# Seven-product FFN tiles: high and low token parts in one matmul, weight totals prepared in DRAM or added by DMA, and a written order

## The chip, the cores and the metric

The kernel runs on one core of a Trainium2 chip. Its time is device microseconds for one launch; three runs gave 2419.32, 2420.54 and 2422.15 us (median 2420.54). The engines are PE (TensorE, matmul; PEld is its weight load), DVE (VectorE), ACT (ScalarE), POOL (GpSimd) and SP (SyncE, which here only issues DMAs). POOL and ACT issue DMAs too; in this kernel the DMAs that add to what stands at their destination are all POOL's.

## The reference

Two layers of an encoder on 512 tokens of width 1024. Each layer has a half-step FFN, a mixer, and another half-step FFN; the change is in the FFNs.

```python
def swiglu(h, w_gate, w_up, w_down):
    return (jax.nn.silu(h @ w_gate) * (h @ w_up)) @ w_down
...
h = rms_norm(x, norm_g[l, 0])
x = x + 0.5 * swiglu(h, ffn_w_gate[l, 0], ffn_w_up[l, 0], ffn_w_down[l, 0])
```

The mixer projects the normalized tokens, runs three kinds of attention beside each other (2-D neighbourhood, differential, windowed with shared keys), gates and merges their outputs, and adds the result to x. The FFN's inner width is 2816, that is 22 tiles of 128 columns.

## The kernel before, in words

**Split numbers.** Everything that TensorE multiplies is split into a high part (rounded to fp32r on ACT) and a low part (the rest, a subtraction on DVE). A product is three matmuls per block of 128 inputs: high weights with high tokens, high weights with low tokens, low weights with high tokens. `parted` (L91) splits a 128x1024 weight tile: one ACT copy (L95) and one DVE subtraction (L96). `weights` (L80) loads a tile and does the same (L86 to L88). Both draw the parts from rings of four buffers (`whi`, `wlo`), and the loaded tile from a ring of three (`raw`).

**The four FFNs.** For each of the 22 tiles `ffn` (L275) computes gate and up. The first two tiles of an FFN (the first four in the first FFN) are plain: 24 matmuls of 512 columns each for gate and for up (`product`, L105), and `gated` (L360) makes silu(gate) times up. During them `Sides` (L368) prepares sums and differences of token blocks. All later tiles, 18 in the first FFN and 20 in each of the other three, go through `seven` (L418).

**A seven-product tile.** Gate and up of one tile are one product of a 2x2 block matrix of weights with a 2x2 block matrix of tokens, and it is done in seven block products instead of eight (Strassen's scheme in Winograd's form). Each block product multiplies 512 inputs with 256 token columns: `block_product` (L456) issues eight matmuls with the high weights (L460, L461) and four with the low ones (L463), all 256 columns wide. The weights of the seven products are: two halves of the raw tile (`wa`), two halves of gate plus up (`w31`, from `wsum`), one quarter of up (`w22`, from `a22`), and two halves of a further total (`w24`). `wsum` is made by two DMAs (`added`, L408): SP loads gate's columns, POOL's DMA adds the up tile (L415). `w24`'s input is made on DVE by two additions of 128x512 into the raw tile (L446, L447), and then parted. The partial sums are gathered from PSUM by ACT copies (L474, L483, L485) and DVE additions (L487, L490, L491); then come the gate's scaling (L494), Silu on ACT (L495), the product (L496) and the split of the result (`keep`, L119 and L121).

**What sets the order.** Within the limits of data and buffers, a planner places each engine's instructions by estimated costs; `tc.issue_after` adds single order constraints. Each engine then works through its list in that order.

**After the tiles** come eight tiles of the down projection (L336 to L348: 66 matmuls of 512 columns each); in the last FFN `finish` (L599) takes their place. The mixer (L666) calls `weights` some 70 times per layer, and POOL in it builds bias tiles (L876, L926) and issues small DMAs, among them the swapped queries `qks` (L700, L701), which the score matmuls read.

## Time and profile before

| what | value |
|---|---|
| three runs | 2419.32, 2420.54, 2422.15 us |
| profiled execution: first to last instruction (its own time; the profile gives no other) | 2419.2 us |
| seven-product tiles of the four FFNs | 54.7 to 238.2, 888.9 to 1090.5, 1233.7 to 1435.3, 2085.9 to 2287.5 us |
| mixers, roughly | 360 to 830 and 1555 to 2030 us |
| busy: PE, DVE, ACT, POOL | 99%, 68%, 52%, 11% |
| granted TensorE clock, mean | 0.998 |
| HBM read, written | 302.69 MB, 12.62 MB |

A row of the timeline has the start in us, the duration in us (a count after it if several are merged), the engine, the line, the operation, what is written and read, and in brackets the idle time before it and what ended that. Matmul records overlap: a matmul's duration runs from its start to the modelled end of its results, and the next one starts well before that. What a matmul costs in a stream is the distance from its start to the next start. The same holds, less strongly, for DVE and ACT. For a DMA the profile gives the time from its issue to its landing.

### The profile page before, as it was taken

To read this page: it belongs to the slowest core of one execution; us is meant where nothing else is said; L and a number is where in the kernel's file an instruction comes from. 1 tells how busy PE (TensorE), PEld (TensorE's weight loads), DVE (VectorE), ACT (ScalarE), POOL (GpSimd) and SP (SyncE) were. 2 spreads that over 40 slices of the span, in tenths; PEclk is the share of its full clock that TensorE was granted. 3 is DMA by queue.
4 is the path that set the end of the run, shared out by engine and by line. 5 is a ranking of instruction groups with operands and counts; after the bars stand their busy time and mean duration, and the time that the engine had idled before them with its cause. 6 is when DMAs were issued, how large, how long until landed. Compare 5 with 4: busy or idle time off the path is not lost.

```text
span 2419.2 us, 37505 instructions
## 1 busy us (share of the span) xinstructions
PE 2404.9 (99%) x14418; PEld 2138.0 (88%) x14418; DVE 1652.9 (68%) x2767; ACT 1254.9 (52%) x2277; POOL 270.2 (11%) x404
## 2 busy tenths in 40 slices
PE   9999999999999999999999999999999999999998
PEld 7999888888888889998899998888888888999987
DVE  7888445766666678884398873467666666888832
ACT  6555225756567445552255552367566674555532
POOL 3100003311000010000010000133110000100000
PEclk9999999999999999999999999999999999999999
DMA  6675444432332457664367754443322324577632
GB/s 198 174 186 162 128 135 124 115 98 80 94 88 80 131 160 183 185 157 143 119 179 183 183 151 131 127 129 104 101 83 87 95 94 131 168 181 182 175 114 70
DMA packets 113298, 327.19 MB, mean 135 GB/s; under 512 B 13464, under 2 KB 18888, under 8 KB 113120
## 3 DMA queue, kind: packets, MB, share of 16 engines
q1 hardware_dynamic: 88896, 247.04, 33.1%
q0 software_dynamic: 23072, 75.90, 14.4%
q8 instruction: 114, 1.87, 0.3%
q10 hardware_dynamic: 1152, 1.86, 0.2%
q14 instruction: 64, 0.52, 0.1%
HBM read 302.69 MB, written 12.62 MB: 130 GB/s over the span
## 4 chain that ended last, share of the span: by engine, by line
PE 98%; ACT 1%; DVE 0%; issue 0%; DMA 0%; SPq 0%; POOLq 0%; POOL 0%; DVEq 0%; ACTq 0%
PE mm L112 9%; PE mm L110 9%; PE mm L109 9%; PE mm L344 5%; PE mm L345 5%; PE mm L347 5%; PE pr L463 5%; PE pr L460 5%; PE mm L460 5%; PE mm L461 5%; PE mm L463 5%; PE pr L461 5%; PE av L847 2%; PE mm L1065 2%; PE mm L1061 2%; PE mm L1060 2%
## 5 line engine op out<-in xcount | busy, mean ns | idle before, releaser
L87 ACT CAST whi<-raw 128x1024 fp32r<-128x1024 f32 (+1 forms) x258 | 265.7, 1031 | 420.9 <-PE mm L345 184.8
L88 DVE TENSOR_TENSOR wlo<-raw,whi 128x1024 fp32r<-128x1024 f32 (+1 forms) x258 | 309.5, 1201 | 229.1 <-ACT whi L87 121.5
L109 PE MATMUL mm<-h,whi 128*128 128x512 f32 x800 | 318.5, 398 | 0.0
L110 PE MATMUL mm<-l,whi 128*128 128x512 f32 x800 | 313.9, 392 | 0.0
L96 DVE TENSOR_TENSOR wlo<-raw,whi 128x1024 fp32r<-128x1024 f32 x156 | 191.1, 1225 | 83.1 <-ACT whi L95 82.9
L345 PE MATMUL mm<-g,whi 128*128 128x512 f32 x528 | 205.4, 389 | 0.0
L344 PE MATMUL mm<-g,whi 128*128 128x512 f32 x528 | 205.4, 389 | 0.0
L112 PE MATMUL mm<-h,wlo 128*128 128x512 f32 x800 | 197.7, 389 | 0.0
L112 PEld LDWEIGHTS mm<-h,wlo 128*128 128x128 f32 x800 | 150.2, 188 | 31.3
L110 PEld LDWEIGHTS mm<-l,whi 128*128 128x128 f32 x800 | 150.5, 188 | 29.1 <-DVE l L141 0.5
L109 PEld LDWEIGHTS mm<-h,whi 128*128 128x128 f32 x800 | 150.4, 188 | 29.0 <-ACT h L139 0.6
L95 ACT CAST whi<-raw 128x1024 fp32r<-128x1024 f32 x156 | 163.9, 1050 | 10.1 <-DMA raw<-in_w_gu 8.0
L460 PE MATMUL pr<-side,whi 128*128 128x256 f32 x624 | 156.5, 283 | 0.0
L461 PE MATMUL pr<-side,whi 128*128 128x256 f32 x624 | 156.5, 283 | 0.0
L461 PE MATMUL mm<-l,whi 128*128 128x256 f32 x624 | 156.5, 283 | 0.0
L460 PE MATMUL mm<-h,whi 128*128 128x256 f32 x624 | 156.4, 283 | 0.0
L415 POOL DMA_DIRECT2D wsum<-in_w_gu x78 | 68.0, 872 | 686.9 <-DVE g L121 255.7
L347 PE MATMUL mm<-g,wlo 128*128 128x512 f32 x528 | 131.4, 389 | 0.0
L474 ACT COPY gu<-mm 128x256 f32<-128x256 f32 x78 | 29.0, 372 | 195.3 <-PE mm L463 195.2
L806 ACT ACTIVATE lg<-lg,negm 128x256 f32<-128x256 f32 (+1 forms) x192 | 114.2, 595 | 26.7 <-DVE negm L803 25.5
L461 PEld LDWEIGHTS mm<-l,whi 128*128 128x128 f32 x624 | 119.8, 192 | 0.2
L460 PEld LDWEIGHTS mm<-h,whi 128*128 128x128 f32 x624 | 119.8, 192 | 0.2
(306 smaller groups left out, 6130.1 us busy)
## 6 DMA issues: line engine op xcount, KB each, us to landing
raw<-in_w_gu SPq DMA_DIRECT2D x94, 512.0 KB, 3.7
wsum<-in_w_gu SPq DMA_DIRECT2D x78, 512.0 KB, 4.1
wsum<-in_w_gu POOLq DMA_DIRECT2D x78, 512.0 KB, 6.6
raw<-in_w_down SPq DMA_DIRECT2D x48, 512.0 KB, 3.6
raw<-in_w_gate SPq DMA_DIRECT2D x48, 512.0 KB, 3.6
raw<-in_w_qk SPq DMA_DIRECT2D x44, 512.0 KB, 3.6
a<-in_w_gu SPq DMA_DIRECT2D x78, 256.0 KB, 4.8
raw<-in_w_branch SPq DMA_DIRECT2D x24, 512.0 KB, 3.5
```

The lines of the kernel that those rows point to most:

```text
L87: nc.scalar.copy(hi[:, w], raw[:, w])
L88: lower[:] = [nc.vector.tensor_tensor(out=lo[:, w], in0=raw[:, w], in1=f(hi[:, w]), op=ALU.subtract).ins]
L96: nc.vector.tensor_tensor(out=lo, in0=src, in1=f(hi), op=ALU.subtract)
L109: nc.tensor.matmul(ps, wh, xhi[k], start=k == 0, stop=False)
L110: nc.tensor.matmul(ps, wh, xlo[k], start=False, stop=False)
L112: nc.tensor.matmul(ps, wl, xhi[k], start=False, stop=k == n - 1)
L344: nc.tensor.matmul(ps, w[k][0], ghi[c + k], start=c + k == 0, stop=False)
L345: nc.tensor.matmul(ps, w[k][0], glo[c + k], start=False, stop=False)
L347: nc.tensor.matmul(ps, w[k][1], ghi[c + k], start=False, stop=c + k == MF - 1)
L460: nc.tensor.matmul(ps, wh[k], bh, start=start and k == 0, stop=False, skip_group_check=True)
L461: nc.tensor.matmul(ps, wh[k], bl, start=False, stop=False, skip_group_check=True)
L463: nc.tensor.matmul(ps, wl[k], bh, start=False, stop=stop and k == 3, skip_group_check=True)
```

## The change

**Joined matmuls.** The high and low parts of the tokens now stand beside each other in one tile ([128, 2, 512], and likewise for the sums and differences). In a "wide" block product one matmul of 2 x 256 columns takes the place of the two with the high weights: the high part's results go to the first half of a PSUM bank, the low part's to the second, and the halves are added later by ACT copies and 256-column DVE additions. The low weights still take 256 columns. Six of the seven products are wide in three FFNs (all but product 1), and products 3, 4 and 5 in the first FFN. A wide product has 8 matmuls instead of 12.

**Weight totals.** For the last three FFNs gate plus up is made ahead, in DRAM, during the mixers (`prepare`): SP copies gate's tile DRAM to DRAM, POOL's DMA adds up's. These steps are handed out by `weights` calls inside the mixer: 40 tiles in the first mixer, 20 in the second. In the tile itself SP loads the finished total. The two additions for `w24` are now two POOL DMAs, SBUF to SBUF, the second on the result of the first; on DVE they remain in the first FFN and in the first tile of each FFN.

**Written order.** Inside `tile` all engines, and the issue of DMAs, follow the order of the program text (`in_order`). Product 4 of a tile, and all that follows from it up to the split of the result (`tail`), is issued inside the next tile, between its products; after the last tile it is issued in the first down tile (or in `finish`). The order of products is 1, 5, 4 of the tile before, 6, 2, 3, 7. The loads of a tile are issued two tiles ahead (one for `a22`). The small tables of the first FFN come inside that order as well.

```diff
+WIDE, WIDE_FIRST = frozenset((2, 3, 4, 5, 6, 7)), frozenset((3, 4, 5))
...
+    owed[0] += owed[1]
+    while ahead and owed[0] >= 1:
+        owed[0] -= 1
+        with tc.issue_after(loaded[0]):
+            if next(ahead[0], ahead) is ahead:
+                ahead.pop(0)
...
-        hi = xpool.tile([P, S], F32R, tag=f"h{k}", name=f"h{k}")
+        both = self.both[k] = xpool.tile([P, 2, S], F32R, tag=f"h{k}", name=f"h{k}")
+        hi, lo = both[:, 0], both[:, 1]
...
+                if m == plain:
+                    tiles = Seven(l, i, h, fp, sides, ghi, glo)
+                    with tc.issue_after(h.marks[1]):
+                        with tc.issue_after(loads[1]):
+                            tiles.fetch(m, sums)
+                        tiles.wa[m] = parted(tiles.raw[m])
+                        tiles.fetch_a22(m)
+                        tiles.fetch(m + 1)
+                        with tc.issue_after(sides[3].mark), tc.issue_after(h.spread):
+                            tiles.w31[m] = parted(sums)
                 with tc.issue_after(h.marks[1]):
-                    held, gated_last = seven(l, i, m, h, fp, sides, ghi, glo, loads[1], sums if m == plain else None, held)
+                    tiles.tile(m)
...
+                if m == 0 and c == 8:
+                    tiles.flush()
...
+        self.t = [two[:, :, :H], two[:, :, H:], both]
+        self.b11, self.b21, self.b22 = h.both[e][:, :, :H], h.both[o][:, :, :H], h.both[o][:, :, H:]
+        self.t4, self.b12 = t4, h.both[e][:, :, H:]
...
+        if (l, i) in prepared:
+            loaded[:] = [nc.sync.dma_start(t, prepared[l, i][m]).ins]
+            return t.rearrange("p n c -> p (n c)")
...
+def prepare(l, i):
+    prepared[l, i] = {}
+    waiting = []
+    def accumulate():
+        t, src = waiting.pop(0)
+        nc.gpsimd.dma_start(t.rearrange("p n c -> p (n c)"), src, accum_op=ALU.add, max_dma_last_dim=4096)
+    for m in range(2, MF):
+        gu = a["w_gu"][l, i, m]
+        t = prepared[l, i][m] = dram.tile([P, 2, S], F32, tag=f"d_s{l}{i}_{m}", name="d_s")
+        nc.sync.dma_start(t, gu.rearrange("n p c -> p n c")[:, :, 0:S])
+        waiting.append((t, gu[1]))
+        if len(waiting) > 2:
+            accumulate()
+        yield
+    while waiting:
+        accumulate()
+        yield
+class Seven:
...
+    @contextmanager
+    def in_order(self):
+        traced = nc.cur_bb.bb.instructions
+        last = traced[-1]
+        yield
+        start = next(k for k in reversed(range(len(traced))) if traced[k] is last) + 1
+        for ins in traced[start:]:
+            if ins.engine in self.behind:
+                why = mybir.DependencyInfo(mybir.DependencyClass.NoSync, mybir.DependencyReason.DATA)
+                tc.add_manual_dep(ins, self.behind[ins.engine].name, why, reason="in_order")
+            self.behind[ins.engine] = ins
+    def fetch(self, m, sums=None):
+        if m >= MF:
+            return
+        (l, i), fp = self.at, self.fp
+        self.sums[m] = sums or added(l, i, m, fp)
+        self.raw[m] = wpool.tile([P, 1024], F32, tag="raw", name="raw", bufs=3)
+        nc.sync.dma_start(self.raw[m], a["w_gu"][l, i, m, 0])
+    def fetch_a22(self, m):
+        if m < MF:
+            self.a22[m] = work.tile([P, S], F32, tag="x", name="a22", bufs=2)
+            nc.sync.dma_start(self.a22[m], a["w_gu"][self.at + (m, 1)][:, S:])
+    def others(self, m, engine):
+        s2, s4 = self.raw[m][:, :S], self.raw[m][:, S:]
+        for out, more in ((s2, self.sums[m][:, S:]), (s4, s2)):
+            if engine is nc.gpsimd:
+                engine.dma_start(out, more, accum_op=ALU.add)
+            else:
+                engine.tensor_tensor(out=out, in0=more, in1=out, op=ALU.add)
+    def product(self, n, bank, w, b, start=False, stop=False):
+        (wh, wl), ps = w, bank[:, 0]
+        for k, bk in enumerate(b):
+            go = start and k == 0
+            if n in self.wide:
+                nc.tensor.matmul(bank, wh[k], bk, start=go, stop=False, skip_group_check=True)
+            else:
+                nc.tensor.matmul(ps, wh[k], bk[:, 0], start=go, stop=False, skip_group_check=True)
+                nc.tensor.matmul(ps, wh[k], bk[:, 1], start=False, stop=False, skip_group_check=True)
+        for k, bk in enumerate(b):
+            nc.tensor.matmul(ps, wl[k], bk[:, 0], start=False, stop=stop and k == 3, skip_group_check=True)
...
+    def tile(self, m):
+        h, fp, sides, last = self.h, self.fp, self.sides, m == MF - 1
+        first = not sides[0].t[3:]
+        tail = iter(self.tail)
+        def rest():
+            for emit in tail:
+                emit()
+                return
...
+        g = quarters(fp)
+        q = [g[:, n] for n in range(5)]
+        one = mm_tile().rearrange("p (a c) -> p a c", a=2)
+        two = psum.tile([P, 2, H], F32, tag="s", name="pr", bufs=2)
+        three = psum.tile([P, 2, H], F32, tag="t", name="pv", bufs=2)
+        wa, w31 = self.wa.pop(m), self.w31.pop(m)
+        w24 = room()
+        with self.in_order():
+            self.fetch(m + 2)
+            self.fetch_a22(m + 1)
+            self.product(1, one, blocks(wa), [s.b11 for s in sides], start=True)
+            rest()
+            if not last:
+                self.wa[m + 1] = room()
+                parted(self.raw[m + 1], self.wa[m + 1])
+                if self.ready:
+                    self.others(m + 1, nc.gpsimd)
+            if first:
+                self.others(m, nc.vector)
+            parted(self.raw.pop(m), w24)
+            rest()
+            u1 = self.halves(1)
+            nc.scalar.copy(g[:, 0:u1], one[:, 0:u1])
+            self.product(5, two, blocks(w31, S), side(1), start=True)
+            rest()
+            if u1 == 2:
+                add(q[0], q[0], q[1])
+            v = self.halves(5)
+            nc.scalar.copy(q[4], two[:, v - 1])
+            if v == 2:
+                add(q[4], two[:, 0], q[4])
+            rest()
+            w22 = [fp.tile([P, S], F32R, tag=t, name=t) for t in ("w22h", "w22l")]
+            a22 = self.a22.pop(m)
+            nc.scalar.copy(w22[0], a22)
+            nc.vector.tensor_tensor(out=w22[1], in0=a22, in1=f(w22[0]), op=ALU.subtract)
+            self.product(6, one, blocks(w24), side(2))
+            u2 = self.halves(1, 6)
+            nc.scalar.copy(g[:, 1 : 1 + u2], one[:, 0:u2])
+            if u2 == 2:
+                add(q[1], q[1], q[2])
+            rest()
+            if first:
+                for s in sides:
+                    s.last()
+            if not last and not self.ready:
+                self.others(m + 1, nc.vector)
+            self.product(2, three, blocks(wa, S), [s.b21 for s in sides], start=True, stop=True)
+            for n in range(self.halves(2)):
+                add(q[0], three[:, n], q[0])
+            if not last:
+                self.w31[m + 1] = room()
+                parted(self.sums.pop(m + 1), self.w31[m + 1])
+            self.product(3, two, blocks(w24, S), [s.b22 for s in sides], stop=True)
+            for n in range(self.halves(3, 5)):
+                add(q[1], two[:, n], q[1])
+            gn = g[:, 0:2].rearrange("p a c -> p (a c)")
+            un = g[:, 3:5].rearrange("p a c -> p (a c)")
+            nc.vector.tensor_tensor(out=gn, in0=gn, in1=h.rb, op=ALU.mult)
+            self.product(7, one, blocks(w31), side(3))
+        u3 = self.halves(1, 6, 7)
+        hi = fp.tile([P, S], F32R, tag="g", name="g", bufs=GBUFS)
+        lo = fp.tile([P, S], F32R, tag="g", name="g", bufs=GBUFS)
+        self.out[0].append(hi)
+        self.out[1].append(lo)
+        def sum22():
+            nc.scalar.copy(g[:, 2 : 2 + u3], one[:, 0:u3])
+            for n in range(u3):
+                add(q[4], q[4], q[2 + n])
+        def gate():
+            nc.scalar.activation(gn, gn, AF.Silu)
+        def fourth():
+            self.product(4, one, blocks(w22), side(4), stop=True)
+        def up():
+            n = self.halves(1, 4, 6, 7)
+            nc.scalar.copy(q[3], one[:, n - 1])
+            if n == 2:
+                add(q[3], one[:, 0], q[3])
+            nc.vector.scalar_tensor_tensor(out=un, in0=un, scalar=-1.0, in1=gn, op0=ALU.mult, op1=ALU.mult)
+        def kept():
+            nc.scalar.copy(hi, un)
+            nc.vector.tensor_tensor(out=lo, in0=un, in1=f(hi), op=ALU.subtract)
+        self.tail = sum22, gate, fourth, up, kept
...
+    ahead[:] = [prepare(*at) for at in ([(0, 1), (1, 0)] if l == 0 else [(1, 1)])]
+    owed[:] = 0.0, 24 * len(ahead) / 72
```

145 lines of the change are left out of this document (49 added, 96 removed).

## The prediction

> **What bounds the kernel now.** I first read the busy shares, the chain of waits, and the table by stretches (us, then busy time and instructions of PE, weight load, DVE, ACT and POOL, granted clock, DMA share, GB/s):
>
> ```profile
> span 2419.2 us, 37505 instructions
> PE 2404.9 (99%) x14418; PEld 2138.0 (88%) x14418; DVE 1652.9 (68%) x2767; ACT 1254.9 (52%) x2277; POOL 270.2 (11%) x404
> PE 98%; ACT 1%; DVE 0%; issue 0%; DMA 0%; SPq 0%; POOLq 0%; POOL 0%; DVEq 0%; ACTq 0%
> ...
> 54.70:238.20 183.50, 182.98 (x1515) 181.78 (x1515) 160.22 (x234) 103.78 (x170) 17.08 (x22) 1.00 0.65 169
> 360.00:830.00 470.00, 469.08 (x2427) 395.29 (x2426) 313.23 (x662) 287.93 (x601) 68.61 (x103) 1.00 0.34 99
> 888.90:1090.50 201.60, 201.60 (x1681) 201.56 (x1680) 175.97 (x243) 112.90 (x184) 16.80 (x20) 1.00 0.67 173
> ```
>
> PE is the bound: almost never idle in the tiles (third and first stretch: 20 tiles of 10.08 us, 18 of 10.19), at full clock. But DVE there is busy 176 of 201.6 us, 87%. So PE time that is taken away counts only until DVE, or something DVE waits for, is the next limit.
>
> A busy PE doesn't yet tell what a matmul costs, since the records overlap. Starts do. PE's timeline, the same product in two successive tiles, and then four 512-column matmuls of the down projection:
>
> ```profile
> 1420.91 0.28 PE L460 MATMUL pv<-h,w22h 128*128 128x256 f32 x1
> 1421.03 0.28 PE L461 MATMUL pv<-l,w22h 128*128 128x256 f32 x1
> ...
> 1430.99 0.28 PE L460 MATMUL pv<-h,w22h 128*128 128x256 f32 x1
> ...
> 1437.84 0.39 PE L345 MATMUL mm<-g,whi 128*128 128x512 f32 x1
> 1438.06 0.39 PE L344 MATMUL mm<-g,whi 128*128 128x512 f32 x1
> 1438.29 0.39 PE L345 MATMUL mm<-g,whi 128*128 128x512 f32 x1
> 1438.52 0.39 PE L344 MATMUL mm<-g,whi 128*128 128x512 f32 x1
> ```
>
> A tile takes 1430.99 - 1420.91 = 10.08 us for 84 matmuls: 0.120 us per 256 columns. At 512 columns it is (1438.52 - 1437.84)/3 = 0.2267 us. The durations in the rows (0.28 and 0.39) would make joining worth 0.17 us a pair; the starts say 2 x 0.120 - 0.2267 = 0.0133 us. The large-looking saving is thirteen times too large.
>
> **The matmuls.** A wide product drops 4 matmuls. Three FFNs: 20 tiles x 6 x 4 x 3 = 1440; the first: 18 x 3 x 4 = 216. Together 1656 x 0.0133 = **22.0 us** less PE time; a tile falls to 9.76 us (a wide product 1.39, product 1 still 1.44), in the first FFN to 9.92. Were joining worth 0.17 us, it would be 280 us; I take the starts, since they add up to the tile's time.
>
> In the Trainium skill, "TensorE: Matmul & The Clock Gate", section "Back-to-back issue gap", a matmul in a stream costs its columns at 2.4 GHz plus 2.5 ns. By that a dropped matmul returns 2.5 ns (an estimate from that page), 1656 of them 4 us, and everything below would turn the change into a loss. This trace differs: 120 ns is 13.3 above 256 columns at that clock, and 227 is 13.3 above 512; the measurement decides.
>
> **DVE and ACT in a tile.** Here too starts count; one tile of DVE, then ACT:
>
> ```profile
> 1393.97 0.42 DVE L487 TENSOR_TENSOR gu<-mm,gu 128x256 f32<-128x256 f32 x1
> 1394.30 1.21 DVE L96 TENSOR_TENSOR wlo<-wsum,whi 128x1024 fp32r<-128x1024 f32 x1
> 1395.44 0.68 DVE L490 TENSOR_TENSOR gu<-pr,gu 128x512 f32<-128x512 f32 x1
> ...
> 1397.24 0.68 DVE L494 TENSOR_TENSOR gu<-gu,rb 128x512 f32<-128x512 f32 x1
> 1397.84 0.68 DVE L447 TENSOR_TENSOR raw<-raw 128x512 f32<-128x512 f32 x1
> ...
> 1391.14 1.05 ACT L95 CAST whi<-raw 128x1024 fp32r<-128x1024 f32 x1
> 1392.09 0.62 ACT L436 CAST w22h<-a 128x512 fp32r<-128x512 f32 x1
> 1392.61 0.37 ACT L485 COPY pv<-pr 128x256 f32<-128x256 f32 x1
> 1392.91 1.04 ACT L95 CAST whi<-wsum 128x1024 fp32r<-128x1024 f32 x1
> ```
>
> DVE needs 1.14 us per 1024 columns, 0.60 per 512, 0.33 per 256; ACT 0.95, 0.52, 0.30. DVE before: three of 1024, eight of 512, one of 256 = 8.55 of 10.08 us. After, in a tile with six wide products: three of 1024, four of 512, nine of 256 (one each for products 1 with 6, 5 and 4, two each for 2, 3 and 7) = 3.42 + 2.40 + 2.97 = 8.79 of 9.76 us. In the first FFN, with L446 and L447 kept and six small additions, 9.0 of 9.92. ACT: 2.85 + 5 x 0.52 + 3 x 0.30 = 6.35. So DVE stays under PE, by a margin reduced from 1.5 to 1.0 us. These additions cost nothing while that cover lasts.
>
> **The two DMA additions.** The input of product 6 (`w24`) now comes from two chained POOL DMAs of 256 KB. Setting the start of a tile to 0, products end at 1.44 (1), 2.83 (5), 4.22 (4 of the tile before), 5.6 (6), 7.0, 8.4, 9.76. On ACT stand first the copy of the last tile's bank (0.2 to 0.7 us), then the rounding of the next tile's raw weights to about 1.8; DVE's subtraction of 1.2 us reads them until 3.0. Only then may the first addition overwrite them. Product 6 of the next tile starts at 9.76 + 4.22 = 13.98; before it ACT must round `w24` (1.05), do the Silu that is queued behind (0.52) and copy product 1 out of product 6's own bank (0.37). So the second addition must land by about 12.0: 9.0 us for two, **4.5 us each**. No such DMA is in the trace. The nearest (KB, median us to landing):
>
> ```profile
> wsum<-in_w_gu POOLq DMA_DIRECT2D x78, 512.0 KB, 6.6
> qks<-qk POOLq DMA_DIRECT2D x72, 128.0 KB, 2.3
> lg<-d_x POOLq DMA_DIRECT2D x16, 256.0 KB, 3.0
> ```
>
> Bounds: 2.3 (half the size, no adding) to 6.6 (twice the size, adding). Plain transfers rise 0.7 from 128 to 256 KB, so plain 512 KB would be 4.4; adding costs 2.2 more there, half of that here: 3.0 + 1.1 = 4.1 us. That is 0.4 us inside the deadline, so it hides; for single late pairs I put 1.2 us in all. At 2.3 us nothing is lost either. With the cover gone, product 6 waits, and behind it all of PE; each us by which one addition exceeds 4.5 us lengthens a tile by about 1 us (both are late, but half is regained, since the next tile's additions start from its raw weights and not from `w24`). At 6.6 that is 60 x 2.1 = 126 us.
>
> **Entry of each FFN.** In its first joined tile product 4 of a tile before is missing, so product 6 is due at 2.83 us, and its input is made on DVE, after the rounding of the next tile's weights. How it looks there now (tile start, then DVE and ACT):
>
> ```profile
> 888.94 0.28 PE L460 MATMUL mm<-h,whi 128*128 128x256 f32 x1
> ...
> 888.37 0.68 DVE L365 TENSOR_TENSOR gu<-pg,gu 128x512 f32<-128x512 f32 x1
> 889.57 0.68 DVE L365 TENSOR_TENSOR gu<-mm,gu 128x512 f32<-128x512 f32 x1
> 891.37 0.68 DVE L121 TENSOR_TENSOR g<-gu,g 128x512 fp32r<-128x512 f32 x1
> 893.51 1.23 DVE L96 TENSOR_TENSOR wlo<-raw,whi 128x1024 fp32r<-128x1024 f32 x1
> ...
> 889.08 0.62 ACT L119 CAST g<-gu 128x512 fp32r<-128x512 f32 x1 [1.11 <-DVE gu L365]
> ```
>
> Now DVE's low part of `w24` ends 5.8 us into the tile, and only the sixth product needs it. After: the next tile's `whi` buffer is the fourth back, that of the last plain product, free at 0.2 us. ACT rounds to 1.25, DVE subtracts to 2.4, adds twice to 3.6, ACT rounds `w24` to 4.7: product 6 waits 2.0 us beyond 2.83, and about 0.3 for the low part. DVE also still owes up to three 512-column steps of the last plain tile (the L365 and L121 rows above), at worst 1.2 us on this path: 2.3 to 3.5. I take 2.6 us x 4 entries = **10.4 us**. PE never regains this. No gain is possible here, since PE loses nothing at this place today; zero is the bound below.
>
> **The preparation in the mixers.** 60 SP copies and 60 POOL additions of 512 KB. A row for all queues' traffic and the price of POOL's part:
>
> ```profile
> q1 hardware_dynamic: 88896, 247.04, 33.1%
> q0 software_dynamic: 23072, 75.90, 14.4%
> ...
> L415 POOL DMA_DIRECT2D wsum<-in_w_gu x78 | 68.0, 872 | 686.9 <-DVE g L121 255.7
> ```
>
> Plain MB cost 0.331 x 2419/247 = 3.24 us of the DMA engines, POOL's 4.6: 4.1 us for one total. 40 totals in the first mixer are 164 of 470 us, and its DMA share goes from 0.34 to about 0.69, no more than the 0.67 at which the tiles above lose nothing. POOL gets 40 x 0.87 = 35 us more beside 69 busy. A weight load behind a copy lands some 2 us later, and is issued a product ahead (24 x 0.227 = 5.4 us); bias builds and swapped queries stand behind additions on POOL's queue. If that cover failed in a third of the cases at 1 us, 20 us; I take 2 us. In the tiles, traffic falls (the total comes in one load instead of two).
>
> **Small tables.** In the first FFN two matmuls now stand in PE's written order and wait for an ACT copy: 1 us, from 0 to 3. Product 4 after the last tile is issued a third into the first down tile (24 x 0.227 = 5.4 us of matmuls before and behind it), longer than its chain: nothing. SP's loads run two tiles ahead: nothing.
>
> **Sum.** 2419.2 - 22.0 + 10.4 + 1.2 + 2 + 1 = 2411.8 us profiled. The runs' median lies 1.3 us above that span, so 2413 us.
>
> **Rivals.**
> - *Nothing lost at the entries*: the planner clears DVE early. For it: DVE has 1.5 us a tile to spare. Against: the written order itself. 2413 - 10 = 2403.
> - *The DMA additions come late*; the slower case. Place: ACT's rounding of `w24`, hence product 6, in 60 tiles. It decides from 4.6 us per addition (60 x 0.12 us eats the 7.4 us gained); at 4.9 us, 60 x 0.4 = 24, less the 1.2 already counted: 2436. For it: 0.4 us is a thin margin, and the loads share the DMA engines. Against: interpolation from three sizes.
> - *The mixers suffer*: 10 us more than I took, 2423.
> - *Joining doesn't do what it says*: moving columns from two separate stretches cost more than the contiguous 512 in the rows, so that a pair takes 0.24 again: 2435. The trace has no such operand in a stream. By the rule of the Trainium skill above it would be 2431; its chance is within this one's.
>
> **How the numbers follow.** Forecast 0.45 (its own range 2406 to 2422), entries free 0.15, late additions 0.2, mixers 0.13, joining worth nothing 0.07. Fewer than 2 in 10 lie outside 2400 (all but the entry cost hidden better than I think) and 2438 (additions at 4.9 us). A measurement tells 0.2% (4.8 us) from no change: faster is below 2415.7, slower above 2425.4. Faster: 0.32 of the forecast's 0.45, and the free entries, 0.47. Slower: 0.16 of the late additions, 0.04 of the mixers, 0.05 of the joining: 0.25. The rest, 0.28, is no change.
>
> **What would show it.** Joined matmuls start 0.227 us apart and a tile lasts 9.76 us: the matmul term holds. PE waits at product 6 for ACT's `w24` only in the first tile of an FFN, 2 to 3.5 us: the entry term. The additions land in about 4.1 us; a PE wait at product 6 in every tile and landings above 4.5 us would be the slower rival. Mixers longer than before with PE waiting for `qks` or raw weights would be the third. I am wrong altogether if DVE, at 90% in a tile, falls behind by itself, shown by PE waiting for DVE where no DMA is late.

## The result, and the profile after

The changed kernel takes **2436.86 us** (median of 4 runs, 2434.38 to 2449.10), the kernel before 2419.93 in the runs beside it: a ratio of **1.0079, with a 95% interval of 1.0055 to 1.0102**. It is slower. The forecast was 2413, faster. The time is inside the range, near its upper end. It is also the value that the rival of the late DMA additions gave (2436), but by coincidence: the sums behind the two differ term by term, as shown below. The profiled run took 2435.98 us with a span of 2433.8, so 14.6 us more span than before, and that is what has to be explained. It is one execution: the four differ by 15 us, since single waits fall differently in each.

First the shares, and the table by stretches of the changed kernel (columns as in the prediction; the third stretch is moved with the tiles):

```profile
span 2433.8 us, 34871 instructions
PE 2401.1 (99%) x12762; PEld 2056.0 (84%) x12762; DVE 1713.3 (70%) x3067; ACT 1323.3 (54%) x2433; POOL 362.4 (15%) x518
...
54.70:238.20 183.50, 179.08 (x1268) 168.64 (x1267) 171.65 (x284) 112.79 (x204) 17.18 (x22) 0.98 0.63 175
360.00:830.00 470.00, 467.04 (x2415) 393.15 (x2414) 317.06 (x661) 287.21 (x600) 93.51 (x141) 1.00 0.68 183
897.00:1098.60 201.60, 198.58 (x1197) 176.18 (x1196) 189.56 (x325) 131.37 (x224) 33.30 (x39) 1.00 0.68 186
```

PE is still the bound by its share, and 1656 matmuls are gone. But it is no longer always busy in the tiles: it misses 4.4 us in the first stretch and 3.0 in the third, where it missed 0.5 and none. DVE has gone from 176 to 190 of 201.6 us, the clock in the first FFN from 1.00 to 0.98. The page's mean busy share of PE, 99% in both, shows none of this. The waits do. The table of PE's waits, after, its largest rows:

```profile
PE mm L518 <- ACT gu L580: 12.8, 8, 3.0
PE mm L520 <- ACT gu L580: 2.4, 1, 2.4
PE st L221 <- DVE parts L218: 2.0, 1, 2.0
```

L518 and L520 are the first matmul of product 6, L580 the copy of product 1, which stands behind the rounding of `w24` in ACT's order, and L221 the small tables' matmul. The first row holds the entries and the late additions, the third the tables, which I had priced; the second, product 6 in the tile behind the tables, I had not. Before, the only wait inside the tiles was 0.5 us. Ten waits make 17.2 us. These rows give PE's idle time by its records; where I give a wait below, I count by how much later than usual the matmul starts, which is some 0.15 us more.

**What joining gives.** PE's timeline in one undisturbed tile, from product 4 to product 4:

```profile
957.08 1.09 PE L518 MATMUL mm<-h,w22h 128*128 128x512 f32 x4
958.01 0.64 PE L523 MATMUL mm<-h,w22l 128*128 128x256 f32 x4
958.49 1.09 PE L518 MATMUL mm<-pair,whi 128*128 128x512 f32 x4
959.41 0.63 PE L523 MATMUL mm<-pair,wlo 128*128 128x256 f32 x4
...
966.94 1.09 PE L518 MATMUL mm<-h,w22h 128*128 128x512 f32 x4
```

The tile lasts 966.94 - 957.08 = 9.86 us, not 9.76: it was 10.08. Four joined matmuls take 958.01 - 957.08 = 0.93 us, 0.232 each and not 0.2267. So a tile gains 0.22 us, not 0.32.

**What a late pair costs.** POOL's additions, SP's loads and PE around 2206 us, in the fourth FFN:

```profile
2196.12 0.87 POOL L507 DMA_DIRECT2D raw<-wsum  x1 [5.28 <-DVE wlo L103]
2201.63 0.86 POOL L507 DMA_DIRECT2D raw<-raw  x1 [4.63 <-DMA raw<-wsum]
```

```profile
2202.16 0.33 SPq L434 DMA_DIRECT2D wsum<-d_s  x1
2202.53 0.43 SPq L494 DMA_DIRECT2D raw<-in_w_gu  x1
2203.00 0.45 SPq L500 DMA_DIRECT2D a<-in_w_gu  x1
```

```profile
2207.70 1.04 ACT L102 CAST whi<-raw 128x1024 fp32r<-128x1024 f32 x1 [3.58 <-DMA raw<-raw]
...
2209.18 0.35 ACT L580 COPY gu<-mm 128x256 f32<-128x256 f32 x1
```

```profile
2206.16 0.64 PE L523 MATMUL mm<-h,w22l 128*128 128x256 f32 x4
2209.59 1.42 PE L518 MATMUL mm<-pair,whi 128*128 128x512 f32 x4 [2.79 <-ACT gu L580]
2210.80 1.05 PE L523 MATMUL mm<-pair,wlo 128*128 128x256 f32 x4
2211.66 1.91 PE L518 MATMUL pv<-h,whi 128*128 128x512 f32 x4
2213.36 0.84 PE L523 MATMUL pv<-h,wlo 128*128 128x256 f32 x4
2214.04 0.85 PE L518 MATMUL pr<-h,whi 128*128 128x512 f32 x3
```

```profile
2209.50:2213.40 3.90, 3.81 (x13) 3.20 (x14) 3.26 (x7) 2.20 (x6) 0.87 (x1) 0.61 0.36 63
```

To be read in this order. The first addition, issued at 2196.12, lands after 5.1 us instead of about 3.4: fifteen of its sixteen parts are there after 3.2 us, one is not. The second can be issued only then, at 2201.63, and half a microsecond behind it SP issues the next tile's three loads, 1.25 MB. It lands after 6.0 us. ACT has sat idle for 3.58 us, rounds `w24` at 2207.70, does the Silu queued behind it, and copies product 1 at 2209.18. PE's product 6 starts 2.95 us late. And then comes what I had not priced: the matmuls behind the wait are slow. Four narrow ones take 2211.66 - 2210.80 = 0.86 us (0.48 in the quiet tile), four joined ones 1.70 (0.93). The granted clock in that stretch, the last fence, is 0.61. For 3.4 us PE runs at half its clock, and that adds 1.66 us.

In the Trainium skill, "TensorE: Matmul & The Clock Gate", section "What's actually happening", the array's clock is halved after an idle window of about 3.4 us and given back after as long a busy one. The length of the slow stretch agrees (3.4 us). But a pause shorter than the window is enough here: 2.1 to 3.1 us in this profile. Where the pause falls matters too, as the last section shows.

**Where the 14.6 us are.** I compared the stages by their number of matmuls (24 of the down projection now stand inside a joined part and are moved back with 5.4 us). The stages are longer than before by: first FFN +4.4 us, second -0.6, third +1.9, fourth +6.7; first mixer +3.1, second +0.5, opening -1.5, end +0.1: 14.6. With the gain of undisturbed tiles taken out (0.22 us in 20 tiles, 0.11 in the first FFN's 18, 15.2 in all), the FFNs lose 6.4, 3.8, 6.3 and 11.1 us, 27.6 together. By place, each wait with the slow clock behind it: the small tables 6.4 (waits of 2.1 and, at product 6 a tile later, 2.6), the entries of the later FFNs 1.4, 6.3 and 1.4, late additions 12.1 (five waits). The tables' and the additions' sums are what is left of an FFN's loss when the rest is taken out, so they hold small losses that I did not place.

### The profile page after: what moved, and what is told of

Read it like the earlier page. It is cut to its first block, busy times and chain, and to the rows that moved or that the text cites. A ratio compares the mean times of both kernels' runs of the same rounds, so it can differ in the third digit from the quotient of the medians.

```text
span 2433.8 us, 34871 instructions
## 1 busy us (share of the span) xinstructions
PE 2401.1 (99%) x12762; PEld 2056.0 (84%) x12762; DVE 1713.3 (70%) x3067; ACT 1323.3 (54%) x2433; POOL 362.4 (15%) x518
## 4 chain that ended last, share of the span: by engine, by line
PE 92%; DVE 2%; DMA 2%; ACT 2%; issue 1%; POOL 0%; SPq 0%; POOLq 0%; ACTq 0%; DVEq 0%
PE mm L117 8%; PE mm L116 8%; PE mm L119 8%; PE mm L518 7%; PE mm L523 6%; PE pr L518 6%; PE mm L364 5%; PE mm L363 5%; PE mm L366 5%; PE pr L523 3%; PE pv L518 2%; PE mm L520 2%; PE mm L521 2%; PE mm L1214 2%; PE mm L1210 2%; PE mm L1209 2%
## 5 line engine op out<-in xcount | busy, mean ns | idle before, releaser
L116 PE MATMUL mm<-h,whi 128*128 128x512 f32 x800 | 318.4, 398 | 0.0
L117 PE MATMUL mm<-h,whi 128*128 128x512 f32 x800 | 313.7, 392 | 0.0
L103 DVE TENSOR_TENSOR wlo<-raw,whi 128x1024 fp32r<-128x1024 f32 x156 | 184.9, 1219 | 15.3 <-ACT whi L102 15.1
L117 PEld LDWEIGHTS mm<-h,whi 128*128 128x128 f32 x800 | 150.5, 188 | 29.0 <-DVE h L148 0.5
L116 PEld LDWEIGHTS mm<-h,whi 128*128 128x128 f32 x800 | 150.4, 188 | 29.0 <-ACT h L147 0.6
L625 ACT COPY gu<-mm 128x512 f32<-128x512 f32 (+1 forms) x78 | 42.0, 538 | 159.1 <-PE mm L523 154.6
L449 POOL DMA_DIRECT2D d_s<-in_w_gu x60 | 51.4, 857 | 474.3 <-DMA d_s<-in_w_gu 415.5
L366 PEld LDWEIGHTS mm<-g,wlo 128*128 128x128 f32 x528 | 99.1, 188 | 20.6
L363 PEld LDWEIGHTS mm<-g,whi 128*128 128x128 f32 x528 | 99.2, 188 | 20.4
L364 PEld LDWEIGHTS mm<-g,whi 128*128 128x128 f32 x528 | 99.1, 188 | 20.4
L556 DVE TENSOR_TENSOR gu<-pr,gu 128x256 f32<-128x256 f32 x234 | 98.1, 419 | 3.6 <-ACT gu L586 1.1
L507 POOL DMA_DIRECT2D raw<-wsum x57 | 49.7, 872 | 322.3 <-DVE wlo L103 289.6
L103 DVE TENSOR_TENSOR wlo<-wsum,whi 128x1024 fp32r<-128x1024 f32 x78 | 94.7, 1215 | 0.0
```

What stands on the lines that cost most here:

```text
L103: nc.vector.tensor_tensor(out=lo, in0=src, in1=f(hi), op=ALU.subtract)
L116: nc.tensor.matmul(ps, wh, xhi[k], start=k == 0, stop=False)
L117: nc.tensor.matmul(ps, wh, xlo[k], start=False, stop=False)
L363: nc.tensor.matmul(ps, w[k][0], ghi[c + k], start=c + k == 0, stop=False)
L364: nc.tensor.matmul(ps, w[k][0], glo[c + k], start=False, stop=False)
L366: nc.tensor.matmul(ps, w[k][1], ghi[c + k], start=False, stop=c + k == MF - 1)
```

## The experiments

They ask whether joining gives something, and whether the loss is single waits of PE with half clock behind the longer ones. Each expectation names the theories that it sets against each other. Times are medians, with the ratio to the kernel before on the same chip and its 95% interval.

| kernel | us | ratio to before |
|---|---|---|
| changed | 2436.9 | 1.0079 (1.0055 to 1.0102) |
| no joining | 2445.9 | 1.0104 (1.0087 to 1.0120) |
| additions issued earlier | 2425.8 | 1.0025 (1.0016 to 1.0034) |
| tables out of the order | 2429.8 | 1.0042 (1.0027 to 1.0056) |
| additions on DVE | 2473.4 | 1.0225 (1.0208 to 1.0242) |
| additions earlier, tables out | 2420.4 | 1.0000 (0.9991 to 1.0010) |
| the same, `w24` rounded first at entries | 2427.1 | 1.0029 (1.0019 to 1.0039) |
| no totals prepared | 2425.0 | 1.0018 (1.0009 to 1.0027) |
| low parts joined too | 2594.2 | one run |
| product 2 ahead at entries | 2434.0 | 1.0065 (1.0049 to 1.0081) |
| earlier, out, and product 2 ahead | 2421.2 | 1.0004 (0.9995 to 1.0013) |
| the same, entry's additions by DMA | 2434.7 | 1.0060 (1.0047 to 1.0072) |
| changed, more loads | 2433.3 | 1.0054 (1.0035 to 1.0074) |

**1. No joining.** The rest of the change as it is, all products with separate matmuls:

```diff
-WIDE, WIDE_FIRST = frozenset((2, 3, 4, 5, 6, 7)), frozenset((3, 4, 5))
+WIDE, WIDE_FIRST = frozenset(), frozenset()
```

> The changed kernel with no joined matmul at all (no block product is wide; all 12 matmuls of 256 columns, as before); the written order, the totals made ahead in DRAM and the two DMA additions stay. Theory A (joining gives about 0.22 us per tile, and the loss comes from the rest of the change: entries, small tables, late additions, preparation): slower than the changed kernel, 2440 to 2452 us, tile period 10.08 us. Theory B (joining itself, with its extra copies and additions, is what makes the kernel slower): near the kernel before, 2418 to 2424 us.

2445.9 us, 9 more than with joining, though the intervals of the two ratios overlap. The tiles are clear: an undisturbed one lasts 10.08 us in this profile and 9.86 in the changed kernel's. Joining does help, so the rival that it does nothing falls. The late additions are there without it too (product 6 of an inner tile waits 3.2 us in the second FFN, 3.3 in the third, 1.5 in the fourth), so they come from the order and the DMAs, not from a tile that became too short. How much joining gives isn't told exactly by this pair's times, since late additions fall differently in each run; the tiles say 0.22 us each.

**2. Additions issued earlier.** The rounding and the subtraction of the next tile's raw weights, and with them the two DMA additions, go ahead of the last tile's copies and of DVE's share of them. A second move is in the same edit: the copy of product 1 goes ahead of the rounding of `w24`:

```diff
-                rest()
                 if not last:
                     self.wa[m + 1] = room()
                     parted(self.raw[m + 1], self.wa[m + 1])
                     if self.ready:
                         self.others(m + 1, nc.gpsimd)
+                rest()
+                u1 = self.halves(1)
+                nc.scalar.copy(g[:, 0:u1], one[:, 0:u1])
                 if first:
                     self.others(m, nc.vector)
                 parted(self.raw.pop(m), w24)
                 rest()
-                u1 = self.halves(1)
-                nc.scalar.copy(g[:, 0:u1], one[:, 0:u1])
```

> The changed kernel with two moves in the written order of a tile: the next tile's raw weights are rounded (and its DMA additions issued) before the last tile's bank is copied, and the copy of product 1 is done before the rounding of product 6's weights. Nothing is added or removed. Theory A (product 6 waits in some tiles because the chain of two DMA additions has no room for one late DMA engine): waits of PE at product 6 inside the FFNs vanish, 2422 to 2430 us. Theory B (these waits come from DVE or ACT being too full): no change, 2434 to 2440 us.

2425.8 us, 11.1 less, and the intervals of the two ratios are apart. Rows of this profile, the waits at product 6 for `w24` and the additions' median landings:

```profile
PE mm L518 <- ACT whi L102: 5.4, 4, 2.6
raw<-wsum POOLq DMA_DIRECT2D x57, 256.0 KB, 3.8
raw<-raw POOLq DMA_DIRECT2D x57, 256.0 KB, 3.3
```

The additions land no sooner (3.8 and 3.3 us against 3.5 and 3.3), but three of the four waits are the entries', and of the waits for an addition in inner tiles only one of 0.5 us is left. That the late additions cost some 12 us is thereby shown: room before the deadline was missing, and the order could give it. Both moves give some. On the median of the tiles without a wait, the first addition is issued 11.3 us ahead of the next product 6 instead of 10.5, and from the second landing to a product 6 that waited for it pass 1.2 us instead of 2.0. No run has one move alone.

**3. The tables out of the written order.** They are still queued behind the instructions before them, but nothing of the tile is ordered behind them:

```diff
-                        with tiles.in_order():
+                        with ExitStack() as behind:
+                            for ins in tiles.behind.values():
+                                behind.enter_context(tc.issue_after(ins))
                             position_tables(fp)
```

> The changed kernel with the small tables of the first FFN queued behind the tile before them, but without the rest of the written order queued behind the tables. Theory A (the two waits of 2.1 and 2.6 us in the first FFN, and the halved clock after each, come from the tables standing in the written order): 2427 to 2433 us. Theory B (they come from the tables' work itself): no change, 2434 to 2440 us.

2429.8 us, 7.0 less; the waits of 2.1 and 2.6 us are gone from the first FFN (1.4 and 1.1 at other places appear). The two small matmuls cost much more than 1 us: 7.0 by the medians, whose intervals just touch, and 4.6 by the length of the first FFN in the two profiles.

**4. Both additions on DVE in every tile.**

```diff
-                    if self.ready:
-                        self.others(m + 1, nc.gpsimd)
...
-                if not last and not self.ready:
+                if not last:
                     self.others(m + 1, nc.vector)
```

> The changed kernel with the two additions for product 6 on DVE in every tile (as in the first FFN) and not by DMA; joins, order and prepared totals stay. Theory A (DVE has no room for 1.2 us more in a tile of 9.86 us): PE waits for DVE in every tile, tile period 10.0 to 10.2 us, 2433 to 2446 us. Theory B (DVE had the room, and only the DMA chain was too slow): tile period 9.86 us without waits, 2422 to 2427 us.

2473.4 us, above what I expected by either theory. PE's waits, first row, and a stretch of tiles:

```profile
PE mm L523 <- DVE wlo L103: 35.6, 54, 1.0
```

```profile
950.00:1050.00 100.00, 94.13 (x558) 80.88 (x556) 98.08 (x168) 62.72 (x105) 0.00 (x0) 1.00 0.36 129
```

PE waits for DVE's low part of `w24` in nearly every tile of the later FFNs, DVE is busy 98 of 100 us, and a tile lasts 10.77 us: DVE is the bound. With six joined products, additions by DMA are needed. The cover under which I put DVE at nothing ends within the 1.2 us of two additions, and it was thinner than I had reckoned: in the changed kernel's tile at 954.80 us DVE's starts add up to 9.6 us and not 8.79, since the nine additions of 256 columns start 0.39 to 0.46 us apart and not 0.33. 9.6 + 1.2 is the 10.8 us of these tiles. Two of the nine in that tile:

```profile
959.13 0.42 DVE L556 TENSOR_TENSOR gu<-mm,gu 128x256 f32<-128x256 f32 x1 [0.24 <-ACT gu L637]
959.59 0.69 DVE L640 SCALAR_TENSOR_TENSOR gu<-gu 128x512 f32<-128x512 f32 x1
...
960.80 0.42 DVE L556 TENSOR_TENSOR gu<-gu 128x256 f32<-128x256 f32 x1
961.22 0.69 DVE L644 TENSOR_TENSOR g<-gu,g 128x512 fp32r<-128x512 f32 x1
```

**5. Both repairs.** The edits of 2 and 3 together.

> The changed kernel with both earlier reorderings: the additions issued before the fourth block product is totalled, and the small tables no longer written into the order. Theory A (the loss is single waits of PE, each followed by a few us of half clock, and the waits of the inner tiles and of the tables are independent): the tables' saving, 7 us, comes on top of the additions' 11, 2417 to 2421 us; left are the waits at the entries of the later FFNs. Theory B (the waits only move: time saved at one place is lost at the next late transfer): no better than the better of the two, 2424 to 2427.

2420.4 us: of 11 and 7 us 16.5 are there together, as with independent waits, and the kernel is level with the one before (1.0000, 0.9991 to 1.0010). What is left in its waits is the entries and the first mixer:

```profile
PE mm L520 <- ACT whi L102: 4.7, 3, 2.6
PE t L988 <- POOL lg L1055: 3.1, 2, 2.9
```

The first mixer is 7.7 us longer than before's in this profile, more than the three entries' waits together; what PE waits for there is told under "Mixers" below.

**6. `w24` first at the entries.** On top of 5, in the first joined tile:

```diff
+                if first:
+                    self.others(m, nc.vector)
+                    parted(self.raw.pop(m), w24)
                 if not last:
                     self.wa[m + 1] = room()
...
-                if first:
-                    self.others(m, nc.vector)
-                parted(self.raw.pop(m), w24)
+                if not first:
+                    parted(self.raw.pop(m), w24)
```

> As the kernel with both reorderings, and in the first joined tile of an FFN the two additions on DVE and the rounding of the input of product 6 stand ahead of the rounding of the next tile's weights. Theory A: the entry waits of 1.1 to 2.8 us in the later FFNs, and the half clock behind them, go (5 to 9 us in three entries), 2409 to 2415 us, faster than the kernel before. Theory B: the additions of the second tile are issued 2.5 us later by this, and land late there, so that the wait moves to product 6 of the second tile: 2417 to 2422.

2427.1 us, slower by 6.7. The waits moved, as theory B said, and grew by more than its numbers (2417 to 2422): the entry wait of the second FFN halves (1.3 to 0.7) and those of the third and fourth become 2.3 and 0, but product 6 of the second tile now waits 3.3 us in the second FFN and 4.7 in the fourth. There the second addition is issued at 899.00 and 2096.41, 0.4 and 0.04 us ahead of SP's loads, and lands after 6.3 and 7.5 us.

**7. No prepared totals.** All FFNs run as the first one:

```diff
-        ahead[:] = [prepare(*at) for at in ([(0, 1), (1, 0)] if l == 0 else [(1, 1)])]
+        ahead[:] = []
```

> The changed kernel without the totals prepared in DRAM: all FFNs run as its first one does, with three joined products, the total by a transfer and an adding transfer, and the two additions on DVE. Theory A: late additions (12 us) and the mixers' share (3.5 us) go, half of the joining's gain is given up (720 of 1656 dropped matmuls x 0.009 = 6.5 us), the entries stay: 2425 to 2430 us, the mixers 3 to 4 us shorter. Theory C (the preparation itself is the loss, 10 us or more in the mixers): the mixers 10 us shorter or more, 2418 to 2423.

2425.0 us, at the lower edge of theory A's numbers. The mixers are 3.0 and 0.2 us shorter than in the changed kernel, so the preparation costs 3 us in the changed kernel's profile and theory C's 10 falls; in the other profiles with the preparation the first mixer was up to 5 us longer again. Without DMA additions no inner tile of the later FFNs waits.

**8. Low parts joined too.** Every matmul of a joined product then has 512 columns:

```diff
+                if n in self.wide:
+                    nc.tensor.matmul(bank, wl[k], bk, start=False, stop=stop and k == 3, skip_group_check=True)
+                else:
-                nc.tensor.matmul(ps, wl[k], bk[:, 0], start=False, stop=stop and k == 3, skip_group_check=True)
+                    nc.tensor.matmul(ps, wl[k], bk[:, 0], start=False, stop=stop and k == 3, skip_group_check=True)
```

> The changed kernel, in which the low parts of the weights in a joined product are multiplied with both token parts as well (their product with the low token part is added, which the kernel leaves out): every matmul of a joined product then has 512 columns, and 1656 x 4 / 4 matmuls grow by 0.107 us, some 177 us in all, so about 2590 us less what the longer tiles hide. Only the distance of the starts is of interest. Theory D (the first matmuls after a change between 256 and 512 columns are the dear ones): inside the tiles the 512-column matmuls now start 0.227 to 0.228 us apart from the second joined product in a row on. Theory E (the two separate stretches of columns, or these banks, cost it): they stay at 0.231 to 0.234 us.

PE's timeline in a tile:

```profile
963.60 1.07 PE L518 MATMUL pv<-h,whi 128*128 128x512 f32 x4
964.51 1.07 PE L524 MATMUL pv<-h,wlo 128*128 128x512 f32 x4
965.42 1.07 PE L518 MATMUL pr<-h,whi 128*128 128x512 f32 x4
966.32 1.07 PE L524 MATMUL pr<-h,wlo 128*128 128x512 f32 x4
```

(966.32 - 963.60)/12 = 0.2267 us, exactly the spacing of the down projection. With the same two-stretch operands and the same banks, theory E falls. What made joined matmuls dear is that each run of four follows four narrow ones: the first eight or so of 512 columns behind a change of size stand 0.228 to 0.236 us apart. In the trace of before, too, the first four of a long product are 0.229 to 0.236 apart and 0.227 is reached from about the eighth.

**9. Product 2 ahead at the entries.** On the changed kernel alone:

```diff
+                if first:
+                    self.product(2, three, blocks(wa, S), [s.b21 for s in sides], start=True, stop=True)
                 self.product(6, one, blocks(w24), side(2))
...
-                self.product(2, three, blocks(wa, S), [s.b21 for s in sides], start=True, stop=True)
+                if not first:
+                    self.product(2, three, blocks(wa, S), [s.b21 for s in sides], start=True, stop=True)
```

> The changed kernel; only in the first joined tile of an FFN product 2, whose inputs are there, is written ahead of product 6. Nothing else is issued earlier or later by it, the second tile's additions least of all. Theory A: each entry's wait becomes 1.4 us shorter, so those of 1.4 us end and the one of 3.1 us falls to 1.7; with the half clock behind the longer one 5 to 7 us less, 2429 to 2432 us. Theory B (waits only move, as they did when the rounding was put ahead): the time that is not waited at the entry is waited at product 6 of the second tile, 2435 to 2437.

2434.0 us, 2.9 less, between the theories, and not clear of the runs' spread; the waits in the profile tell more. The three entry waits become 0, 1.7 and 0, as A said. But in the second tile PE now waits 1.0 to 1.1 us for DVE, which hasn't made the low part of `w24` (L523 <- wlo L103). Of 1.4 us given to an entry, 1.1 are taken back.

**10. Product 2 ahead, on top of 5.**

> The kernel with both reorderings (additions earlier, tables out of the order; 2420 us), and product 2 ahead of product 6 in the first joined tile of an FFN. Theory A: the entry waits of 1.3, 2.8 and 1.1 us fall to 0, 1.4 and 0, with the clock behind the longest 5 us less: 2414 to 2417 us, faster than the kernel before by 0.1 to 0.3%. Theory B: 2419 to 2422, since the second tile waits instead.

2421.2 us, theory B: no better than without it (2420.4). PE's largest row of waits is now DVE's:

```profile
PE mm L525 <- DVE wlo L103: 5.2, 5, 1.1
```

**11. The entry's additions by DMA as well,** to relieve DVE there, on top of 10:

```diff
                             tiles.wa[m] = parted(tiles.raw[m])
+                            if tiles.ready:
+                                tiles.others(m, nc.gpsimd)
...
-                if first:
+                if first and not self.ready:
                     self.others(m, nc.vector)
```

> As the kernel with both reorderings and product 2 ahead (2421 us), and the two additions of the first joined tile of the later FFNs, too, are done by adding transfers, issued when that tile's raw weights have been parted, before the tile starts; that takes 1.2 us from DVE in the first tile. Theory A (DVE, behind after the entry, makes the second tile wait 1.2 us for a low part): those waits go, 3 to 4 us in three entries, if the two transfers take the 7.2 us that they take elsewhere and there are that many before the rounding: 2416 to 2418 us. Theory B: the transfers, issued beside the loads of the next tiles, land late, and the wait at the first product 6 is back with 1 to 3 us and its half clock: 2421 to 2427.

2434.7 us: theory B's mechanism, at a higher price than its 2421 to 2427. At each of the three entries the second addition is issued together with SP's loads; POOL's and SP's rows at the third FFN:

```profile
1239.69 0.93 POOL L511 DMA_DIRECT2D raw<-wsum  x1 [7.55 <-ACT pair L422]
1243.45 0.86 POOL L511 DMA_DIRECT2D raw<-raw  x1 [2.83 <-DMA raw<-wsum]
...
1252.77 0.85 POOL L511 DMA_DIRECT2D raw<-raw  x1 [5.49 <-DMA raw<-wsum]
```

```profile
1243.08 0.33 SPq L438 DMA_DIRECT2D wsum<-d_s  x1
1243.45 0.43 SPq L498 DMA_DIRECT2D raw<-in_w_gu  x1
1244.00 0.35 SPq L504 DMA_DIRECT2D a<-in_w_gu  x1
```

The second addition lands 7.6 us after 1243.45, and product 6 waits 4.3 us; in the other two FFNs 5.2 and 3.8.

**12. More loads.** The changed kernel, with the 256 KB load of product 4's weights made twice:

```diff
-                nc.sync.dma_start(self.a22[m], a["w_gu"][self.at + (m, 1)][:, S:])
+                for _ in range(2):
+                    nc.sync.dma_start(self.a22[m], a["w_gu"][self.at + (m, 1)][:, S:])
```

> The changed kernel, in which the 256 KB load of the weights of product 4 is made twice, one behind the other: the loads of a tile become 1.5 MB instead of 1.25 MB and go on 2 to 4 us into the time of the additions; the result is the same. Theory F (additions are late when they share the transfer engines with the next tiles' loads): their median landing rises from 3.4 us to 4 us or more, and product 6 waits in many tiles: 2450 to 2500 us. Theory G (only single events, such as the fetching of instructions, make an addition late): the median stays within 0.2 us of 3.4, the time within 5 us of 2437.

2433.3 us, within 5 us of the changed kernel, and the additions' median is 3.5 us against 3.4: theory G. DMA engines that are busier by a tenth (share 0.76 against 0.69 in the second FFN's tiles) don't by themselves make additions late.

**What makes an addition late,** from ten profiles of these kernels together: second additions, by how long behind them the 512 KB load of raw weights is issued.

| load issued behind the second addition by | landing, us |
|---|---|
| 0.0 us (3 cases) | 7.5 to 7.7 |
| 0.4 | 7.5 |
| 0.6 (2) | 6.6 and 6.7 |
| 0.7 to 0.9 (6) | 5.7 to 6.3 |
| 1.05 to 1.2 (4) | 4.2 to 5.0 |
| 1.3 to 1.5 (6) | 3.6 to 4.1 |
| none within that (551) | median 3.3, longest 6.3 |

Nothing that was run moves the loads alone; but the order is the same in all ten profiles, and the kernels of experiments 6 and 11 brought the two together by their order and paid for it. So what counts, as far as these runs go, is less the amount of traffic than the coincidence with one burst. Why a first addition sometimes comes late, as at 2196.12, and thereby brings the second to the burst, stays open. In the ten profiles, of 391 transfers of POOL into `raw` with an instruction fetch in their first 3.2 us, 157 had one of their sixteen parts more than 0.4 us behind the other fifteen; of the 755 others, 62. That goes together; no run changed the fetching, so it is not shown to be the cause.

## Why the prediction was wrong, by its steps

**The two DMA additions: the step that failed.** I took 4.1 us for one, a deadline of 4.5, and 1.2 us "for single late pairs". The landing was estimated too high (the median is 3.4 us), and still the loss was 12.1 us; experiment 2, with more room, takes 11.1 off. The fault was to set a typical landing against a deadline, and to price what lies beyond it at 1.2 us without a row for it. The deadline was too generous as well: the first addition is issued 3.6 us into a tile and not 3.0, and 0.4 us, which I left out, pass from its landing to the second issue. From the first issue to the next product 6 are 10.5 us on the median, the work behind the second landing takes 2.0, and a median pair takes 7.3: that leaves 1.2 us for both together. A pair that meets the next burst of loads takes 11.5 (5.1 + 0.4 + 6.0), and POOL's chain makes the second pay for the first. "The loads share the DMA engines" stood in the rival, and a collision with loads is what the late rows show; its condition, 4.9 us in all 60 tiles, was not met. Five late pairs cost 12.1 us, not its 24, part of that by a price that I left out: the half clock behind a wait of over 2 us. That the whole time came out at the rival's 2436 is luck.

**The matmuls: right mechanism, a size off.** -22.0 us was -15.2. Reading the starts and not the durations was right, and so was that joining helps (experiment 1); but the quoted rows came from the middle of a long product, and joined matmuls come in fours. 2 x 0.120 - 0.232 is 0.008 us; with the narrow ones behind the joined, slightly closer together, 15.2/1656 = 0.0092 us for a dropped matmul, not 0.0133. The Trainium skill gives 2.5 ns per matmul for back-to-back ones in "TensorE: Matmul & The Clock Gate", section "Wait — 56ns, not 53.3ns?"; its section "Back-to-back issue gap", which the prediction names, calls the same formula that of an isolated matmul. The 4 us estimated from that page are further off than the 22. In the first FFN the 9.92 us per tile started from 10.08 and not from the 10.19 read off beside it; undisturbed tiles there went from 10.08 to 9.96.

**Entries: near in sum by luck, wrong in places.** 10.4 us was 9.1: nothing at the first FFN, and 1.4, 3.1 (3.5 with the step behind it) and 1.4 of waits at the others, 6.3 together, and 2.8 for the half clock behind the longest, which I had not priced. "PE never regains this" holds; experiments 6, 9 and 10 show that it can hardly be bought off either, since DVE, the additions and the loads stand close behind.

**Small tables:** 1 us, "from 0 to 3", was up to 6.4 (all that the first FFN lost); experiment 3 says 4.6 to 7.0. I counted the wait for the copy, and not that an order written out on all engines hands it on: product 6 of the next tile waits again, 2.6 us, and in this profile the clock falls behind each.

**DVE at nothing:** right in the tiles, where no wait on DVE shows in the changed kernel, though its sum was 0.8 us a tile too small. But its cover has no second use: experiment 4 spends 1.2 us of it and loses 37 us, experiments 9 and 10 find DVE behind in the second tile of each FFN.

**Mixers:** 2 us was 3.6, and 3.2 by experiment 7. PE's largest wait there is for a MEMSET in the attention, which stands behind the additions on POOL's queue:

```profile
429.64 0.83 POOL L449 DMA_DIRECT2D d_s<-in_w_gu  x1 [8.15 <-DMA d_s<-in_w_gu]
432.53 0.41 POOL L1053 MEMSET lg<- 128x128 f32 x2
432.85 0.55 PE L986 MATMUL t<-ident,lg 128*128 128x128 f32 x3 [0.86 <-POOL lg L1053]
```

POOL stands 8.15 us at a prepared addition, until SP's copy has landed. Behind it come four copies of queries and the MEMSET, and only then PE's transpose, which reads what the MEMSET writes. PE has two such waits here, 1.4 us together. The two profiles without the preparation (before, and experiment 7) have none; in experiment 5's the longest is 2.9 us and in experiment 12's 4.0. In the twelve profiles with it the first mixer is 0.9 to 8.0 us longer than before's, so the 3.1 here is one draw of a term that varies and that I had put too low; how much of it these waits make is shown only for the two above. The first mixer's DMA share was 0.68; the forecast of about 0.69 was above the tiles' 0.67 and not within it. The copies of swapped queries took 6.1 us instead of 2.3, as feared; their users did not wait:

```profile
qks<-qk POOLq DMA_DIRECT2D x72, 128.0 KB, 6.1
raw<-wsum POOLq DMA_DIRECT2D x57, 256.0 KB, 3.5
raw<-raw POOLq DMA_DIRECT2D x57, 256.0 KB, 3.3
```

Together: -15.2 + 12.1 + 9.1 + 6.4 + 3.6 - 1.5 (opening, which the change doesn't touch) + 0.1 = 14.6 us. The forecast had -7.4. Of the 22 us between the two the additions are 10.9, the matmuls 6.8, the tables 5.4 and the mixers 1.6; the entries and the opening go the other way. No kernel among those run is faster than the one before: with additions earlier and the tables out it is level, and what joining gives there goes on the mixers, the entries and the waits that are left.

## What to carry to other kernels

A transfer that must land within a tile is to be set against the deadline with its latest landing, not its median, and with what else is issued in the same microsecond; if there is no room, issue it earlier in the order and shorten what follows its landing, which here together gave back 11 of 12 us with no more work. Price a wait of PE of over 2 us with 1.7 us on top for each 3.4 us of half clock that it may bring. Take the spacing of matmuls from runs as long as those that the change will make.

## What the runs showed of the hardware that I had not expected

- PE's clock is halved by waits shorter than 3.4 us, and it depends on where a wait falls. In the tiles of eleven profiles, of 29 waits from 2.1 to 3.3 us 22 were followed by a slow stretch. In each of the fourteen profiles all changes of the clock stand whole multiples of 3.41 us apart. If the time is cut into such stretches, from 10 us after the start to 25 us before the end, 34 of those at full clock were followed by one at half. In 33 of them PE was idle for 1.87 us or more (in one for 1.49), and in none of the 9801 others for more than 1.88. At the third entry PE idles for 2.64 us in experiments 2 and 5 alike: in 2 all of it lies in one stretch, and the clock halves; in 5 it is split into 1.62 and 1.02, and it does not.
- After a change from 256 to 512 columns matmuls start 0.228 to 0.236 us apart, 0.227 only from about the eighth (experiment 8).
- An adding transfer of 256 KB inside SBUF lands in 3.3 us on the median, and in up to 7.7 when 1.25 MB of loads are issued at the same moment; the same loads begun 3.8 us ahead of it, as in most tiles, leave it at 3.5, and begun 3.0 us ahead, in experiment 2, at 3.8.
- An addition on POOL's queue that waits for its copy holds up the work behind it: after 8.15 us of such a wait PE stood 0.86 us for a MEMSET (the mixers above).
